# Hybrid decoder block on one core: the sixteen rows of modulation section 4 with four buffers, loaded ahead of their products

## The chip, the cores and the metric

The kernel runs on one core of one Trainium2 chip. The metric is the device time of one execution in microseconds, the median of several runs. The engines are named as the profile names them: PE is TensorE (its weight loads are PEld), DVE is VectorE, ACT is ScalarE, POOL is GpSimd, SP is SyncE, which here only issues transfers.

## The reference, cut to what matters

One layer of width 2048 over 512 positions, in f32. The vector `mod` has six sections of 2048; section 4 is the scale of the second norm.

```python
mod = jax.nn.silu(c) @ w_ada[l] + b_ada[l]
sh1, sc1, ga1, sh2, sc2, ga2 = jnp.split(mod, 6, axis=-1)
h = modulate(rmsnorm(x, g_mix_norm[l]), sh1, sc1)
proj = h @ w_in[l]
...
y = jnp.concatenate([rmsnorm(y_ssm, g_ssm_out[l]), rmsnorm(y_att, g_nsa_out[l])], axis=-1) @ w_out[l]
x = x + ga1[:, None, :] * y
h = modulate(rmsnorm(x, g_ffn_norm[l]), sh2, sc2)
x = x + ga2[:, None, :] * conv_ffn(h, w_up[l], conv_w[l], conv_b[l], w_down[l])
return rmsnorm(x, g_final)
```

`modulate(h, shift, scale)` is `h * (1 + scale) + shift`; `conv_ffn` is up projection, a causal convolution of width 3, gating, down projection.

## The kernel before

Activations lie transposed: 128 channels on the partitions, 512 positions along a row, so x is 16 tiles of 128 by 512. Every matrix product with exact weights is three matmuls (`mm3`, L100 to L102): a weight block is split by ACT into a rounded part `wh` (a cast) and by DVE into the rest `wl` (a subtraction), both L75, and the same is done to the activations (`yh`, `yl`).

The stages follow each other: `phase_a` and `phase_b1` (first modulation, input projection, state space part), `phase_b2` (attention, with the first half of the output projection as fill), `phase_c` (second half of the output projection, residual x, sums of squares), `up_first` and `up_rest` (up projection), `down`.

The change lies in `phase_c`. For its 16 output tiles it multiplies the attention half of the output projection's weights (`wout`) with `yh` and `yl`. The first two tiles (`first`) are made while DVE scales the last part of `yatt` by the norm's factor `rba` (L1055) and splits it. Two accumulators `mm` in PSUM are used in turn: the matmuls of tile n wait until `add` (L1043, on DVE) has read tile n-2 out of its accumulator into x, and for the `wl` and `wh` of their own tile, which have two places each as well. After `add`, ACT squares x (`cv`, L966), DVE adds the squares (L967), and a transfer on POOL's queue writes x to DRAM (`x2_d`, L1045).

In the same stage the 2048 numbers of section 4 are made: 16 rows of 128 numbers. For each row a block of w_ada (128 by 2048, f32, 1024 KB) is loaded into `adw`, DVE multiplies it with `silc` (silu of c, on every partition) and sums along the row (L124, result `adac`), and a one-column instruction (L333) writes `mod`. `adw` has two places. Rows 0 and 1 are loaded on SP's queue before the loop and multiplied there; the rest are loaded on POOL's queue, one behind each output tile, and the program text puts a row's product right behind its load.

All is written for one scheduler that orders each engine's instructions by the program's order and its own estimate of when inputs are there; each engine then works strictly in that order, and so does each queue of transfers. So an instruction that waits for its operand holds all that stands behind it on its engine. POOL's queue also holds the small power `rms_r` (L146) on which `rba` depends.

Of the kernel before, what the change touches and what calls it, by code (L numbers as in the profile page):

```python
# [10 lines left out]
F32 = mybir.dt.float32  # L11
# [3 lines left out]
ALU = mybir.AluOpType  # L15
# [3 lines left out]
P = 128  # L19
D = 2048  # L20
S = 512
KT = D // P
# [42 lines left out]
class Block:  # L65
# [262 lines left out]
    def ada_rest(self, sec, kt, pool=None, bufs=2, late=False):  # L328
        acc = self.cp.tile([P, 1], F32, name="adac", bufs=4)
        self.ada(sec, kt, acc, pool, bufs, late)  # L330
        o = self.mod[:, sec, kt:kt + 1]
        if sec == 4:
            self.V.scalar_tensor_tensor(o, acc, self.vec(V_GFFN + kt), self.mad[:, sec, kt:kt + 1],  # L333
                                        op0=ALU.mult, op1=ALU.add)
        else:
            self.V.tensor_add(o, acc, self.mad[:, sec, kt:kt + 1])
# [691 lines left out]
    def phase_c(self, x2, yatt, yh, yl, W, Wa, ps):  # L1028
        nc, tc, a, V, A, T = self.nc, self.tc, self.a, self.V, self.A, self.T

        Wa.tile([P, 2048], F32, name="adw", bufs=2)
        W.tile([P, S], F32, name="cv", bufs=CVB)
        W.tile([P, 8, P], F32R, name="rh", bufs=2)
        W.tile([P, 8, P], F32R, name="rl", bufs=2)
        na = sum(ADA) - 32
        for i in range(2):
            self.ada_rest(4, na, Wa, 2)
            na += 1
        for q in range(4):
            nc.sync.dma_start(x2[q], self.x_d[:, 4 * q:4 * q + 4])  # L1040
        def add(mt, p, sl):
            x = x2[mt // 4][:, mt % 4, sl]
            V.scalar_tensor_tensor(x, p, self.mod[:, 2, mt:mt + 1], x, op0=ALU.mult, op1=ALU.add)  # L1043
            self.add_square(self.acc2[:, sl], x, mt == 0, W)
            nc.gpsimd.dma_start(self.x2_d[:, mt, sl], x)  # L1045

        def first():

            w = self.weights(a["wout"][0, 1, 0])
            p = [ps.tile([P, S], F32, name="mm", bufs=2) for _ in range(2)]  # L1050
            for f in range(2):
                sl = slice(256 * f, 256 * f + 256)
                for k in range(8):
                    y = yatt[:, k, sl]
                    V.scalar_tensor_tensor(y, y, self.vec(V_GNSA + k), self.rba[f], op0=ALU.mult, op1=ALU.mult)  # L1055
                    self.split(y, yh[:, k, sl], yl[:, k, sl])
                    for e, (wh, wl) in enumerate(w):
                        self.mm3(p[e][:, sl], (wh[:, k], wl[:, k]), (yh[:, k, sl], yl[:, k, sl]), k == 0, k == 7)
            return p

        for u in range(7):
            for e, p in enumerate(self.wout_pair(u, 1, yh, yl, ps) if u else first()):
                add(2 * u + e, p, slice(0, S))
                if na < KT and 2 * u + e >= 0:
                    self.ada_rest(4, na, Wa, 2)
                    na += 1
        nc.sync.dma_start(self.taps, a["taps"])
        V.tensor_scalar(self.tapn, self.taps[:, NFF:, 0:3], -1.0, None, op0=ALU.mult)

        w = self.weights(a["wout"][3, 1, 1])  # L1070
        for f in range(2):
            sl = slice(256 * f, 256 * f + 256)
            for e, (wh, wl) in enumerate(w):
                p = ps.tile([P, 4, P], F32, name="tp", bufs=3).rearrange("p a b -> p (a b)")[:, sl]
                for k in range(8):
                    self.mm3(p, (wh[:, k], wl[:, k]), (yh[:, k, sl], yl[:, k, sl]), k == 0, k == 7)
                add(14 + e, p, sl)
                if f:
                    self.norm2(e, ps, W)
                    if e == 0:  # L1080
                        self.eps0 = self.rms_eps
# [457 lines left out]
```

## Time and profile before

| | |
|---|---|
| runs | 2338.4, 2343.06, 2365.14 us |
| median | 2343.06 us |
| profiled execution | 2354.09 us, its span 2352.3 us |
| busy in the span | PE 2195.6, PEld 1918.0, DVE 1854.9, ACT 1080.2, POOL 309.6 us |
| granted TensorE clock, mean | 0.967 of full speed |
| `phase_c`'s stretch, 846 to 947 us | PE 79.91, DVE 75.78, ACT 25.31 of 101 us |

The page of the profile gives busy time by engine and by group of instructions; the views used below are the waits (who waited for whom), the timeline of one engine, sums over given stretches, and the issues of transfers with the time until they landed. In a timeline a row is the start, the duration, the engine, the line, and in brackets the idle time ahead of it with what ended it; consecutive rows overlap in the pipeline, so the step from one start to the next is what an instruction costs.

### The profile page before, as it was taken

The page shows a single profiled execution, that of the slowest core. Times are in us where ns is not written, and L with a number is a line of the kernel's source. Part 1 is how long each engine was busy: PE and PEld are TensorE (multiplying, and loading weights), DVE is VectorE, ACT ScalarE, POOL GpSimd, SP SyncE. Part 2 cuts the span into 40 slices and gives each one's busy share as a digit, 9 for nine tenths or more (in the row PEclk, how much of TensorE's full clock was granted, in tenths as well). Part 3 has the DMA queues.
Part 4 walks back from the last instruction along what each step waited for, and adds up shares of the span by engine and source line. Part 5 has one row for each costly group of instructions (what it writes and reads, how often), then busy time and mean ns, then how long its engine had stood idle before and what let it go on. Part 6 is the DMA issues. An engine that isn't in the chain of part 4 may idle for free.

```text
span 2352.3 us, 34734 instructions
## 1 busy us (share of the span) xinstructions
PE 2195.6 (93%) x13694; PEld 1918.0 (82%) x13694; DVE 1854.9 (79%) x2776; ACT 1080.2 (46%) x1823; POOL 309.6 (13%) x376
## 2 busy tenths in 40 slices
PE   7997899878899878899999999999999999999997
PEld 5776778666677666899999999999999788888886
DVE  7896888658988877889999999999999773553436
ACT  3422444348867742744445444454444431221215
POOL 8999111100000011000000000000000000000000
PEclk9999999979999989999999999999999999999998
DMA  9784656576477467233333333333333783443223
GB/s 345 289 284 177 207 167 177 158 209 207 150 239 228 171 258 287 85 123 127 126 129 126 122 122 122 122 121 122 122 121 112 286 310 120 148 145 119 90 90 108
DMA packets 94003, 398.20 MB, mean 169 GB/s; under 512 B 19968, under 2 KB 28448, under 8 KB 58384
## 3 DMA queue, kind: packets, MB, share of 16 engines
q1 hardware_dynamic: 79440, 344.51, 42.0%
q0 software_dynamic: 14400, 51.49, 6.6%
q8 instruction: 107, 1.75, 0.3%
q14 instruction: 56, 0.46, 0.1%
HBM read 358.20 MB, written 37.69 MB: 168 GB/s over the span
## 4 chain that ended last, share of the span: by engine, by line
PE 54%; issue 4%; DVE 3%; ACT 1%; DMA 1%; POOL 1%; POOLq 0%; DVEq 0%; ACTq 0%
PE dn L102 7%; PE dn L100 7%; PE dn L101 6%; PE sa L101 6%; PE sa L100 6%; PE sa L102 6%; PE sb L100 5%; PE sb L102 5%; PE sb L101 5%; DMA adw<-in_wada_dram 0%; DVE wl L75 0%; DMA a_d<-cv 0%; POOL adw L119 0%; POOL x_d L1045 0%; DVE cv L1090 0%
## 5 line engine op out<-in xcount | busy, mean ns | idle before, releaser
L75 ACT CAST wh<-wr 128x1024 fp32r<-128x1024 f32 (+1 forms) x257 | 262.0, 1024 | 502.5 <-PE dn L101 320.5
L75 DVE TENSOR_TENSOR wl<-wr,wh 128x1024 fp32r<-128x1024 f32 (+1 forms) x255 | 307.6, 1210 | 50.1 <-ACT wh L75 38.8
L124 DVE SCALAR_TENSOR_TENSOR adw<-adw,silc 128x2048 f32<-128x2048 f32 x63 | 146.7, 2331 | 26.4 <-DMA adw<-in_wada_dram 25.3
L100 PE MATMUL mm<-yh,wh 128*128 128x512 f32 (+1 forms) x320 | 129.4, 409 | 26.7 <-DVE x L1043 7.8
L75 ACT CAST xh<-wq 128x1024 fp32r<-128x1024 f32 x84 | 88.3, 1052 | 139.2 <-DVE wq L1229 104.2
L75 ACT CAST wh<-wq 128x1024 fp32r<-128x1024 f32 x84 | 88.3, 1052 | 137.8 <-DVE wq L1229 104.5
L1099 POOL DMA_DIRECT2D a_d<-cv x44 | 23.8, 541 | 856.5 <-DVE cv L1098 856.5
L101 PE MATMUL mm<-yl,wh 128*128 128x512 f32 (+1 forms) x320 | 128.8, 403 | 7.4 <-DVE yl L75 7.4
L102 PE MATMUL mm<-yh,wl 128*128 128x512 f32 (+1 forms) x320 | 127.9, 401 | 1.9 <-DVE wl L75 1.9
L1293 DVE SCALAR_TENSOR_TENSOR x<-dn,mod,x 128x512 f32<-128x512 f32 (+1 forms) x56 | 37.6, 673 | 108.3 <-PE dn L102 107.8
L75 DVE TENSOR_TENSOR xl<-wq,xh 128x1024 fp32r<-128x1024 f32 x84 | 102.4, 1218 | 24.2 <-ACT xh L75 24.2
L75 DVE TENSOR_TENSOR wl<-wq,wh 128x1024 fp32r<-128x1024 f32 x84 | 102.2, 1218 | 22.7 <-ACT wh L75 22.7
L100 PE MATMUL dn<-b21h,wh 128*128 128x512 f32 x256 | 101.8, 398 | 3.1 <-ACT wh L75 3.1
L102 PE MATMUL dn<-b21h,wl 128*128 128x512 f32 x256 | 102.1, 399 | 0.5 <-DVE wl L75 0.5
L1229 DVE TENSOR_TENSOR wq<-wq,wr 128x1024 f32<-128x1024 f32 x84 | 102.0, 1215 | 0.1
L101 PE MATMUL dn<-b21l,wh 128*128 128x512 f32 x256 | 101.8, 398 | 0.0
L100 PE MATMUL dn<-t4h,wh 128*128 128x512 f32 (+1 forms) x256 | 97.8, 382 | 0.0
L102 PE MATMUL dn<-t4h,wl 128*128 128x512 f32 (+1 forms) x256 | 97.7, 382 | 0.0
L101 PE MATMUL dn<-t4l,wh 128*128 128x512 f32 (+1 forms) x256 | 97.6, 381 | 0.0
L100 PEld LDWEIGHTS mm<-yh,wh 128*128 128x128 f32 x320 | 62.7, 198 | 41.7 <-issue 16.9
L146 POOL TENSOR_TENSOR rms_r<-rms_v,mhalf 128x2 f32<-128x2 f32 (+1 forms) x8 | 10.8, 1346 | 637.5 <-DVE rms_v L144 637.4
L102 PE MATMUL mm<-hh,wl 128*128 128x512 f32 x192 | 79.5, 414 | 15.9 <-DVE wl L75 15.9
(535 smaller groups left out, 7852.8 us busy)
## 6 DMA issues: line engine op xcount, KB each, us to landing
adw<-in_wada_dram SPq DMA_DIRECT2D x49, 1024.0 KB, 6.7
wr<-in_wup_dram SPq DMA_DIRECT2D x46, 1024.0 KB, 4.9
wq<-in_wup_dram SPq DMA_DIRECT2D x42, 1024.0 KB, 6.8
wr<-in_wdn_dram SPq DMA_DIRECT2D x40, 1024.0 KB, 4.9
wr<-in_wada_dram SPq DMA_DIRECT2D x32, 1024.0 KB, 4.9
wr<-in_wout_dram SPq DMA_DIRECT2D x16, 1024.0 KB, 5.5
adw<-in_wada_dram POOLq DMA_DIRECT2D x14, 1024.0 KB, 7.7
wr<-in_wp_dram SPq DMA_DIRECT2D x12, 1024.0 KB, 5.2
```

The source lines that it names most:

```text
L75: return self.A.copy(hi, src), self.V.tensor_sub(lo, src, hi.bitcast(F32))
L100: self.T.matmul(ps, wh, xh, start=start, stop=False)
L101: self.T.matmul(ps, wh, xl, start=False, stop=False)
L102: self.T.matmul(ps, wl, xh, start=False, stop=stop)
L124: self.V.scalar_tensor_tensor(t, t, 1.0, self.silc, op0=ALU.mult, op1=ALU.mult, accum_out=out)
L146: self.rms_pow = self.nc.gpsimd.tensor_tensor(r[:, 0:n], v[:, 0:n], self.mhalf.to_broadcast([P, n]), op=ALU.pow)
L1099: self.nc.gpsimd.dma_start(self.a_d[:, m], val)
L1229: V.tensor_add(src, src, add)
L1293: V.scalar_tensor_tensor(x, p, gate, x, op0=ALU.mult, op1=ALU.add)
```

## The change

`adw` gets four places. Four rows are loaded before the loop, all on POOL's queue. Behind each output tile the oldest loaded row is multiplied and another is loaded; behind the last two tiles of the loop two rows are multiplied. The products and their number stay.

```diff
+    def ada_load(self, sec, kt, pool, bufs):
+        t = pool.tile([P, 2048], F32, name="adw", bufs=bufs)
+        self.nc.gpsimd.dma_start(t, self.a["wada"][sec, kt])
+        return sec, kt, t
+
+    def ada_row(self, sec, kt, t):
+        acc = self.cp.tile([P, 1], F32, name="adac", bufs=4)
+        self.V.scalar_tensor_tensor(t, t, 1.0, self.silc, op0=ALU.mult, op1=ALU.mult, accum_out=acc)
+        self.ada_out(sec, kt, acc)
...
-        Wa.tile([P, 2048], F32, name="adw", bufs=2)
+        Wa.tile([P, 2048], F32, name="adw", bufs=4)
...
-        for i in range(2):
-            self.ada_rest(4, na, Wa, 2)
-            na += 1
+        rows = []
+
+        def row():
+
+            nonlocal na
+            if na < KT:
+                rows.append(self.ada_load(4, na, Wa, 4))
+                na += 1
+
+        for i in range(4):
+            row()
...
                 add(2 * u + e, p, slice(0, S))
-                if na < KT and 2 * u + e >= 0:
-                    self.ada_rest(4, na, Wa, 2)
-                    na += 1
+                self.ada_row(*rows.pop(0))
+                if u == 6:
+                    self.ada_row(*rows.pop(0))
+                row()
```

`ada_out` holds the one-column instruction that stood in `ada_rest`. In the changed file L124 becomes L340 for these rows, L119 becomes L335, L333 becomes L346, L1043 becomes L1064, L1055 becomes L1076, L1045 becomes L1066.

On DVE, at the end of `first` and the first two tiles, the order before is this (`yatt` and `yl` are the last pieces of the scaled attention output, `adw,adac` is a row's product, `x_7650` the tiles of x):

```order
L75 TENSOR_TENSOR yl<-yatt,yh 128x256
L124 SCALAR_TENSOR_TENSOR adw,adac<-adw,silc 128x2048
L1055 SCALAR_TENSOR_TENSOR yatt<-yatt,vecs,rba_3953 128x256
L333 SCALAR_TENSOR_TENSOR mod<-adac,vecs,mad 128x1
L1055 SCALAR_TENSOR_TENSOR yatt<-yatt,vecs,rba_3953 128x256
L75 TENSOR_TENSOR yl<-yatt,yh 128x256 x2
L124 SCALAR_TENSOR_TENSOR adw,adac<-adw,silc 128x2048
L75 TENSOR_TENSOR wl<-wr,wh 128x1024 x2
L1043 SCALAR_TENSOR_TENSOR x_7650<-mm,mod,x_7650 128x512
```

Three products stand ahead of the first two `wl`; the third is that of row 2, whose load is issued behind the product of row 0. In the changed kernel the same place on DVE reads:

```order
L75 TENSOR_TENSOR yl<-yatt,yh 128x256 x3
L1076 SCALAR_TENSOR_TENSOR yatt<-yatt,vecs,rba_3953 128x256 x2
L340 SCALAR_TENSOR_TENSOR adw,adac<-adw,silc 128x2048
L75 TENSOR_TENSOR yl<-yatt,yh 128x256 x2
L346 SCALAR_TENSOR_TENSOR mod<-adac,vecs,mad 128x1
L340 SCALAR_TENSOR_TENSOR adw,adac<-adw,silc 128x2048
L75 TENSOR_TENSOR wl<-wr,wh 128x1024 x2
L1064 SCALAR_TENSOR_TENSOR x_7650<-mm,mod,x_7650 128x512 x2
L346 SCALAR_TENSOR_TENSOR mod<-adac,vecs,mad 128x1
L340 SCALAR_TENSOR_TENSOR adw,adac<-adw,silc 128x2048
L980 TENSOR_TENSOR acc_7654<-acc_7654,cv 128x512
```

Two products, of rows 0 and 1, stand ahead of the `wl`, and that of row 2 has moved behind the two `add`. Behind these rows the scheduler puts rows 3 and 4 ahead of the `add` of tile 2, so that by tile 11 all sixteen are done; the number of instructions on DVE is the same.

On POOL's queue the place around the last `rms_r` of the attention's norm reads before (`x_d<-z` and `x_d<-x_7650` are stores of x):

```order
L1009 DMA x_d<-z 128x512 x2
L146 TENSOR_TENSOR rms_r<-rms_v,mhalf 128x2
L119 DMA adw<-in_wada_dram 128x2048 x3
L1045 DMA x_d<-x_7650 128x512 x2
L119 DMA adw<-in_wada_dram 128x2048 x2
```

And in the changed kernel:

```order
L1022 DMA x_d<-z 128x512 x2
L335 DMA adw<-in_wada_dram 128x2048
L146 TENSOR_TENSOR rms_r<-rms_v,mhalf 128x2
L335 DMA adw<-in_wada_dram 128x2048 x5
L1066 DMA x_d<-x_7650 128x512 x2
```

The load of row 0 now stands on POOL ahead of `rms_r`, those of rows 1 to 5 behind it; on SP's queue the two loads that stood ahead of the four loads of x (L1040) are gone. PE's, ACT's and the rest of SP's order stay, but for one place: the two matmuls that spread `rms_r` stand eight small matmuls later on PE.

## Rows read from the trace of the kernel before

**Rows 1.** The page: busy time of PE over the span.

```profile
PE 2195.6 (93%) x13694; PEld 1918.0 (82%) x13694; DVE 1854.9 (79%) x2776; ACT 1080.2 (46%) x1823; POOL 309.6 (13%) x376
```

**Rows 2.** Stretches: us, busy of PE, PEld, DVE, ACT, POOL, PEclk, DMA share, GB/s.

```profile
846.00:947.00 101.00, 79.91 (x339) 63.65 (x340) 75.78 (x103) 25.31 (x36) 14.73 (x27) 0.90 0.74 274
...
1010.00:1780.00 770.00, 764.93 (x6620) 756.66 (x6619) 717.86 (x790) 382.14 (x438) 21.63 (x40) 1.00 0.34 124
...
866.00:947.00 81.00, 71.83 (x291) 56.66 (x292) 60.34 (x76) 20.22 (x26) 13.06 (x24) 0.94 0.73 271
```

**Rows 3.** Waits of PE, then of DVE, 846 to 950: total us, times, longest.

```profile
PE mm L100 <- DVE x L1043: 7.8, 1, 7.8
PE mm L100 <- DVE mod L333: 7.6, 2, 6.0
...
PE mm L102 <- DVE wl L75: 1.6, 1, 1.6
...
DVE adw L124 <- DMA adw<-in_wada_dram: 16.9, 7, 5.8
```

**Rows 4.** Timeline of DVE, 845 to 866.

```profile
845.29 1.28 DVE L1055 SCALAR_TENSOR_TENSOR yatt<-yatt,vecs,rba 128x256 f32<-128x256 f32 x3 [2.01 <-ACT rba L938]
846.48 1.09 DVE L75 TENSOR_TENSOR yl<-yatt,yh 128x256 fp32r<-128x256 f32 x3
847.49 1.27 DVE L1055 SCALAR_TENSOR_TENSOR yatt<-yatt,vecs,rba 128x256 f32<-128x256 f32 x3
...
860.60 2.29 DVE L124 SCALAR_TENSOR_TENSOR adw<-adw,silc 128x2048 f32<-128x2048 f32 x1 [4.46 <-DMA adw<-in_wada_dram]
...
862.82 2.35 DVE L75 TENSOR_TENSOR wl<-wr,wh 128x1024 fp32r<-128x1024 f32 x2
865.09 0.74 DVE L1043 SCALAR_TENSOR_TENSOR x<-mm,mod,x 128x512 f32<-128x512 f32 x1
```

**Rows 5.** Timeline of PE, 865 to 947.

```profile
865.98 0.77 PE L100 MATMUL mm<-yh,wh 128*128 128x512 f32 x1 [7.81 <-DVE x L1043]
...
869.67 0.39 PE L100 MATMUL mm<-yh,wh 128*128 128x512 f32 x1
...
933.62 0.77 PE L100 MATMUL mm<-yh,wh 128*128 128x512 f32 x1 [6.01 <-DVE mod L333]
...
937.60 0.39 PE L100 MATMUL mm<-yh,wh 128*128 128x512 f32 x1
...
946.70 0.28 PE L100 MATMUL tp<-yh,wh 128*128 128x256 f32 x1
```

**Rows 6.** Stretches of 2 us: PE busy, PEclk, DMA share, GB/s.

```profile
856.00:858.00 2.00, 2.00 (x10) 0.50 0.96 303
...
874.00:876.00 2.00, 2.00 (x11) 1.00 1.05 442
```

**Rows 7.** Timeline of POOL and of SP around the first loads.

```profile
843.36 0.72 POOL L146 TENSOR_TENSOR rms_r<-rms_v,mhalf 128x2 f32<-128x2 f32 x1 [8.72 <-DVE rms_v L144]
851.95 0.59 POOL L119 DMA_DIRECT2D adw<-in_wada_dram  x1 [7.88 <-issue]
...
836.83 0.91 SPq L119 DMA_DIRECT2D adw<-in_wada_dram  x2
```

**Rows 8.** Queues of transfers, 866 to 947: packets, MB, share of 16 engines' time.

```profile
q0 software_dynamic: 2722, 15.62, 51.2%
q1 hardware_dynamic: 864, 6.29, 21.4%
```

**Rows 9.** POOL's loads: landing of those at 851.95, 880.06, 919.59; time on POOL.

```profile
adw<-in_wada_dram POOLq DMA_DIRECT2D x1, 1024.0 KB, 8.6
...
adw<-in_wada_dram POOLq DMA_DIRECT2D x1, 1024.0 KB, 5.0
...
adw<-in_wada_dram POOLq DMA_DIRECT2D x1, 1024.0 KB, 9.8
...
L119 POOL DMA_DIRECT2D adw<-in_wada_dram x14: 537/539/587, 852.0 to 919.6; - x14
```

More of the change, by code (lines that the diff above doesn't have):

```diff
@@ L330, in ada_rest, with ada_out @@
         self.ada(sec, kt, acc, pool, bufs, late)
+        self.ada_out(sec, kt, acc)
[6 more added lines that the diff above has]
+        self.V.scalar_tensor_tensor(t, t, 1.0, self.silc, op0=ALU.mult, op1=ALU.mult, accum_out=acc)
+        self.ada_out(sec, kt, acc)
+    def ada_out(self, sec, kt, acc):
         o = self.mod[:, sec, kt:kt + 1]
```

## The prediction

> **What bounds the kernel now.** I read the page first: PE is busy for 93% of the span [rows 1], and in the long up projection for 764.93 of 770 us [rows 2]. So time is lost where PE stands, and `phase_c` is such a place: from 846 to 947 PE is busy for 79.91 of 101 us, at a mean clock of 0.90 [rows 2]. Work behind this stage follows PE and should move with it.
>
> Next the waits of PE in that stretch [rows 3]. The two long ones, 7.8 and 6.0 us, are both charged to DVE: in the first PE waits for the `add` of tile 0, which frees its accumulator, in the second for the `add` of tile 10. Two shorter ones of 1.6 us (the rest of the 7.6, and the wait for `wl`) are DVE's too. DVE itself waited 16.9 us for loads of `adw`, seven times, at most 5.8 us. The timeline of DVE shows how these hang together [rows 4]: the product of row 2 stands still for 4.46 us until 860.60, the two `wl` and the `add` of tile 0 (865.09) stand behind it, and PE starts at 865.98 [rows 5]. The load of that row was issued at 851.95 [rows 7], behind the product of row 0 whose place it takes, and took 8.6 us [rows 9]. The load at 919.59 took 9.8 us, and from that come the 5.8 us of DVE and the 6.0 us of PE.
>
> Each long wait costs twice: PE comes back at half its clock, which is 1.2 instead of 2.4 GHz (0.50 in 856 to 858 [rows 6]). At full clock a matmul of 512 columns costs 0.233 us (39 of them from 937.60 to 946.70). The nine from 865.98 to 869.67 took 3.69 us instead of 2.10, the nine from 933.62 to 937.60 took 3.98 [rows 5]: 1.6 and 1.9 us lost.
>
> **The start: tile 0 to the first matmul of tile 2.** Before, PE starts tile 2 at 865.98. In the changed order two products, not three, stand ahead of the `wl`, and neither waits if its row has landed. DVE then works without a stop from the arrival of `rba`, 845.29. From [rows 4]: three scalings of `yatt` in 1.19 us, so eight in 3.2; three `yl` in 1.01, so eight in 2.7; two products at 2.22 (860.60 to 862.82), 4.4; the two `wl` 2.27; a one-column step 0.1. That is 12.7 us, 858.0 for the start of the `add`. The spread of `rms_r` stands eight small matmuls later on PE; half of 0.233 each would be 0.9 us, but PE had been standing for `rms_r` there, so I take 0.3, with 0 and 0.9 as ends. The `add` begins at 858.3, and as PE followed it by 0.89 us before (865.09 to 865.98), tile 2 begins at 859.2. **Gain 6.8 us**; 6.2 to 7.1.
>
> Are the operands there? Row 0 stood on SP until 836.83 [rows 7], for transposes whose input lay in its place. On POOL its load waits for the same, and `rms_r`, now behind it, began at 843.36, so 6 us cover it. Row 0 is multiplied at about 850.8. Row 1 stands behind `rms_r`, is issued at 844.2, and must be there at 853.7: 9.5 us, where the loads shown took 5.0 to 9.8 [rows 9]. x is loaded on SP without the two rows ahead of it.
>
> **The loop: tiles 2 to 13.** Before, from 865.98 to 946.70 they take 80.7 us [rows 5]. 12 tiles of 24 matmuls at 0.233 are 67.2. The difference, 13.5, is 6.2 of gap ahead of 933.62, some 1.8 for each of the two short ones, 1.6 and 1.9 at half clock, and 0.2 left over. After, no gap should be left: rows are loaded four ahead, and DVE's work fits. In 866 to 947 DVE was busy for 60.34 us [rows 2] with 13 products; one more makes 62.6, less than 67.2. Going through the new order by these durations, the closest place is behind each pair of products (rows 6 and 7, rows 10 and 11), where `wl` and `add` still come about 2 us ahead of PE. PE still stands some 4.6 us ahead of tile 2, so I keep 1.7 us for a start at half clock: 68.9 us, end at 928.1. **Gain of the loop 11.8 us**, 18.6 with the start.
>
> **What the transfers allow.** The text says about three tiles from load to product; the scheduler pulls products forward, so row 4 is multiplied straight behind row 3, about 12 us behind its load (853.1 to 865.0). And the stage asks for the same bytes in less time. From [rows 8]: POOL's queue took 41.5 us (51.2% of 81) for 15.62 MB, 2.66 us each MB; SP's 17.3 us for 6.29 MB, 2.75 each. A row (1.05 MB) is 2.8 us, a weight block 2.9, a store of x 0.7. From 844, when row 1 is issued, to 914, when the product of row 15 would start, there are 15 rows (42 us), 5 weight blocks (14.5), 11 stores (7.7) and about 2 MB left of x (5.6): 69.8 us of work in 70. So the queues are as good as full. It may still fit, since row 15 can be 4 us late before PE notices, and since a share of 1.05 at 442 GB/s occurs [rows 6]. The cost of this lies between 0 and 4.5 us; I take 0.6, near the lower end, as PE has 2 to 4 us in hand at each place.
>
> Sum: 18.0 us. The profiled execution took 2354.09, 11 above the median; it would take 2336.1. From the median of 2343.06, **2325 us**. That is 0.8%; about 1%, 23.4 us, is what a measurement of this kernel can tell from no change, as its three runs spread over 27 us.
>
> **One rule against the change.** Two rows move from SP's queue to POOL's. The 14 loads on POOL took 537 to 587 ns each, beside an almost busy DVE [rows 9]. The Trainium skill, "SBUF — State Buffer", section "A bandwidth-pool intuition that's wrong (but worth ruling out)", says that a POOL-issued transfer of about 620 ns took about 3100 ns beside a DVE copy, since GpSimd can't write its descriptors until DVE releases the port that they share. By that row 1 would be issued and land about 2.6 us later, some of it behind DVE's demand, and the time would be up to 2327.6. The trace does not show it: the longest of the 14 is 587 ns.
>
> **Rivals.** *Rows late (0.22).* The full queues make DVE wait again, now for a backlog of three rows: row 4, then the second of each pair. For it: 69.8 in 70 us, and 303 GB/s at a share of 0.96 with two rows on POOL's queue [rows 6]. Against: each row is asked for only when an older product is done, so the backlog can't grow. Here too belongs row 1, if it lands at 844.2 + 14 instead of 9.5: 4.5 us at the start. Price 3 to 7 us: 2328 to 2332.
>
> *Slower: the transfers become the bound (0.04).* If a MB in this stretch costs not 2.7 but over 3.4 us (below about 295 GB/s), the 69.8 us become 88, the last product comes 18 us later, and all is given back; at 4 us, 103, it is 15 us slower: 2358. The 303 GB/s of one slice stand near that point, but 442 in another and 271 on average with idle time against it.
>
> *The change doesn't reach PE (0.06).* If the order of DVE leaves some other wait ahead of the `add` of tile 0 (x's own load, the `wout` block), the gaps move and stay: 2338 to 2345. Against it: before, 16.9 us of DVE's waits were for `adw` and none for these.
>
> *More than this (0.04).* If PE comes back at full clock and no load is late, 20.3 and a half more where the loads of the up projection come sooner: 2322.
>
> **How the numbers follow.** The forecast itself has 0.64, 2320 to 2330. Runs spread by some 6 us to each side of a median, so the range that holds 8 in 10 goes from 2314 to 2339: it takes in the rows that come late and leaves out the transfers as bound and half of the change that doesn't reach. Faster by over 1% (below 2319.6) needs a measurement 5 us below the forecast or the better case: 0.22. Slower by over 1%: 0.03. Within 1%: 0.75.
>
> **What would show it.** In the changed trace the `add` of tile 0 begins at about 858, PE starts tile 2 at about 859, no product of rows 0 to 2 waits for its load, and the small accumulators `tp` begin near 928 to 930. PE's waits on DVE in the loop (7.8, 6.0, 1.6, 1.6) shrink to one of some 4.6 ahead of tile 2; PE's clock is low once, not twice. The DMA share between 845 and 915 rises from 0.74 to over 0.9. Behind the stage every distance stays: the span behind the first `tp` was 2352.3 - 946.7 = 1405.6 us. I am wrong if the product of row 1 or row 4 stands for more than 3 us, if gaps of PE remain in the loop, or if a later stage takes back what this one gave.

## The result, and the profile after

The changed kernel takes 2334.43 us (median of 18 runs, 2326.87 to 2340.27), the kernel before, run beside it, 2349.7 us (18 runs, 2338.4 to 2365.14): a ratio of 0.9933, 95% interval 0.9918 to 0.9947, or 15.3 us less. The forecast was 2325 us (18.0 us less), the range 2314 to 2339. The profiled execution took 2332.81 us, its span is 2331.0 us.

Busy time of PE on the page, and then sums over stretches (columns as in [rows 2]); the stretch of `phase_c` first, then the time in which the rows are loaded:

```profile
PE 2186.7 (94%) x13694; PEld 1909.0 (82%) x13694; DVE 1855.1 (80%) x2776; ACT 1080.8 (46%) x1823; POOL 312.0 (13%) x378
```

```profile
846.00:947.00 101.00, 88.56 (x446) 73.92 (x446) 88.88 (x127) 34.40 (x51) 18.29 (x32) 0.95 0.78 303
...
845.00:915.00 70.00, 62.99 (x284) 51.15 (x285) 68.73 (x94) 21.46 (x30) 12.67 (x24) 0.95 0.94 369
```

In the kernel before, the second stretch reads:

```profile
845.00:915.00 70.00, 54.59 (x241) 43.52 (x240) 56.64 (x78) 17.46 (x26) 11.48 (x21) 0.90 0.83 312
```

In the same 101 us PE does 446 matmuls where it did 339 [rows 2], some of them the shorter ones of the work that follows. The waits of PE in this stretch show why (total us, times, longest; those of the norm behind the first `tp` are left out):

```profile
PE mm L100 <- DVE x L1064: 4.4, 1, 4.4
...
PE mm L101 <- DVE yl L75: 1.9, 2, 1.7
PE mm L100 <- ACT yh L75: 1.4, 1, 1.4
```

Of the four waits on DVE in [rows 3] one is left, 4.4 us ahead of tile 2; those for `yl` and `yh` belong to tiles 0 and 1 and stood before as well (1.8 and 2.7 us). And of DVE's own waits, 16.9 us for `adw` before, none is left at all: the view has no such line any more. The timeline of DVE shows the new start (compare [rows 4]):

```profile
844.77 1.28 DVE L1076 SCALAR_TENSOR_TENSOR yatt<-yatt,vecs,rba 128x256 f32<-128x256 f32 x3 [2.02 <-ACT rba L951]
...
849.96 2.29 DVE L340 SCALAR_TENSOR_TENSOR adw<-adw,silc 128x2048 f32<-128x2048 f32 x1
...
853.07 2.29 DVE L340 SCALAR_TENSOR_TENSOR adw<-adw,silc 128x2048 f32<-128x2048 f32 x1
...
855.29 2.36 DVE L75 TENSOR_TENSOR wl<-wr,wh 128x1024 fp32r<-128x1024 f32 x2
857.56 1.41 DVE L1064 SCALAR_TENSOR_TENSOR x<-mm,mod,x 128x512 f32<-128x512 f32 x2
...
859.01 2.29 DVE L340 SCALAR_TENSOR_TENSOR adw<-adw,silc 128x2048 f32<-128x2048 f32 x1
...
861.96 2.29 DVE L340 SCALAR_TENSOR_TENSOR adw<-adw,silc 128x2048 f32<-128x2048 f32 x1
...
864.16 2.29 DVE L340 SCALAR_TENSOR_TENSOR adw<-adw,silc 128x2048 f32<-128x2048 f32 x1
...
913.48 2.28 DVE L340 SCALAR_TENSOR_TENSOR adw<-adw,silc 128x2048 f32<-128x2048 f32 x1
```

Up to 866 no row has brackets behind it but the first: DVE never stands still here. The `add` of tile 0 comes 12.79 us behind the arrival of `rba` (857.56 - 844.77); before it was 19.80 (865.09 - 845.29). PE, from its timeline (compare [rows 5]), starts tile 2 at 858.45, is slow for nine matmuls (3.76 us until 862.21), and reaches the first `tp` at 927.31 without another gap:

```profile
858.45 0.77 PE L100 MATMUL mm<-yh,wh 128*128 128x512 f32 x1 [4.39 <-DVE x L1064]
...
862.21 0.39 PE L100 MATMUL mm<-yh,wh 128*128 128x512 f32 x1
...
927.31 0.28 PE L100 MATMUL tp<-yh,wh 128*128 128x256 f32 x1
```

The clock of these places, in stretches of 2 us (compare [rows 6]), is low once and not twice: it is back at full from 862 and stays there up to the first `tp`.

```profile
856.00:858.00 2.00, 0.00 (x0) 0.00 (x0) 2.00 (x3) 0.00 (x0) 0.21 (x1) 0.50 0.97 406
...
862.00:864.00 2.00, 2.00 (x10) 1.63 (x9) 2.00 (x2) 0.00 (x0) 0.15 (x1) 1.00 0.99 414
```

On POOL the load of row 0 is issued at 836.80, the rows 1 to 3 directly behind `rms_r`, and row 4 behind the product of row 0 (timeline of POOL, compare [rows 7]):

```profile
836.80 0.55 POOL L335 DMA_DIRECT2D adw<-in_wada_dram  x1 [2.67 <-PE pv L937]
842.84 0.72 POOL L146 TENSOR_TENSOR rms_r<-rms_v,mhalf 128x2 f32<-128x2 f32 x1 [5.49 <-DVE rms_v L144]
843.52 1.65 POOL L335 DMA_DIRECT2D adw<-in_wada_dram  x3
852.55 0.54 POOL L335 DMA_DIRECT2D adw<-in_wada_dram  x1 [7.38 <-DVE adw L340]
```

The load of row 1, issued at 843.52, with the time to its landing, and all sixteen loads with the time that their issue took on POOL:

```profile
adw<-in_wada_dram POOLq DMA_DIRECT2D x1, 1024.0 KB, 9.5
...
L335 POOL DMA_DIRECT2D adw<-in_wada_dram x16: 537/538/587, 836.8 to 896.9; - x16
```

Row 1 thus landed at about 853.05, and its product began at 853.07: no wait shows, but there was nothing to spare either. The rows 2 to 15 landed 2.4 us or more ahead of their products.

**Where the time came from.** The stage runs from the arrival of `rba` on DVE to the first `tp` on PE: 101.41 us before (845.29 to 946.70), 82.54 after (844.77 to 927.31), 18.87 less. Of these the start gave 7.01 (20.69 to 13.68 us from `rba` to tile 2) and the loop of twelve tiles 11.86 (80.72 to 68.86). The two profiled executions differ by 21.3 us in span, though: 0.5 was there when `rba` came, and behind the first `tp` the distance to the end is 1403.7 us for 1405.6. The experiments show that the other 2 us are no part of the change, and why the medians differ by 15 and not by 19.

### The profile page after: what moved, and what is told of

Its sections match the earlier page's. It is cut to its first block, busy times and chain, and to the rows that moved or that the text cites. A ratio compares the mean times of both kernels' runs of the same rounds, so it can differ in the third digit from the quotient of the medians.

```text
span 2331.0 us, 34737 instructions
## 1 busy us (share of the span) xinstructions
PE 2186.7 (94%) x13694; PEld 1909.0 (82%) x13694; DVE 1855.1 (80%) x2776; ACT 1080.8 (46%) x1823; POOL 312.0 (13%) x378
## 4 chain that ended last, share of the span: by engine, by line
PE 71%; DVE 11%; POOL 6%; ACT 4%; DMA 4%; issue 4%; SPq 0%; DVEq 0%; POOLq 0%; ACTq 0%
PE dn L102 6%; PE dn L100 6%; PE dn L101 6%; PE sa L100 6%; PE sa L101 6%; PE sa L102 6%; PE sb L100 5%; PE sb L102 5%; PE sb L101 5%; POOL sp L59 3%; PE mm L100 3%; PE mm L102 3%; PE mm L101 3%; DVE wl L75 2%; PE s L900 1%
## 5 line engine op out<-in xcount | busy, mean ns | idle before, releaser
L75 ACT CAST wh<-wr 128x1024 fp32r<-128x1024 f32 (+1 forms) x257 | 262.0, 1024 | 515.8 <-PE dn L101 320.7
L124 DVE SCALAR_TENSOR_TENSOR adw<-adw,silc 128x2048 f32<-128x2048 f32 x47 | 111.0, 2364 | 7.6 <-DMA adw<-in_wada_dram 6.4
L1309 DVE TENSOR_TENSOR x<-x,dn 128x512 f32<-128x512 f32 x32 | 22.0, 686 | 91.6 <-PE dn L102 91.6
```

Of the source, the lines that this page charges most:

```text
L75: return self.A.copy(hi, src), self.V.tensor_sub(lo, src, hi.bitcast(F32))
L124: self.V.scalar_tensor_tensor(t, t, 1.0, self.silc, op0=ALU.mult, op1=ALU.mult, accum_out=out)
L1309: V.tensor_add(x, x, p)
```

## The experiments

My theory: with two places a load is issued only behind the product of two rows before, so DVE waits for landings; in the start one product stood ahead of the `add` of tile 0 that had no need to. Rivals: only the order of the products counts, or only the number of places, or the queue that rows 0 and 1 are on; the transfers cost something that no wait shows, or set the end themselves.

All times of the stage are read as above, from the timelines of DVE and PE, in us behind the arrival of `rba`. The loop is the time from tile 2 to the first `tp`. Ratios are to the kernel before on the same chip.

| kernel | `add` 0 | tile 2 | first `tp` | loop | ratio, interval |
|---|---|---|---|---|---|
| before | 19.80 | 20.69 | 101.41 | 80.72 | |
| before_again | 17.52 | 18.41 | 97.57 | 79.16 | |
| before_third | 18.52 | 19.41 | 97.47 | 78.06 | |
| changed | 12.79 | 13.68 | 82.54 | 68.86 | 0.9933, 0.9918 to 0.9947 |
| changed_again | 12.68 | 13.57 | 82.76 | 69.19 | 0.9953, 0.9933 to 0.9973 |
| two_places | 12.68 | 13.57 | 91.25 | 77.69 | 0.9979, 0.9961 to 0.9997 |
| three_places | 12.69 | 13.58 | 82.64 | 69.06 | 0.9931, 0.9910 to 0.9952 |
| rows01_on_sp | 12.68 | 13.57 | 82.74 | 69.17 | 0.9930, 0.9910 to 0.9950 |
| four_places_old_text | 18.86 | 19.75 | 89.16 | 69.42 | 0.9981, 0.9962 to 0.9999 |
| four_places_old_text_again | 19.31 | 20.20 | 89.58 | 69.38 | |
| no_reload | 12.80 | 13.69 | 82.91 | 69.22 | 0.9934, 0.9901 to 0.9967 |
| rows_twice | 12.81 | 13.70 | 86.64 | 72.94 | 1.0026, 1.0005 to 1.0047 |
| adds_first | 7.05 | 8.03 | 76.01 | 67.98 | 0.9910, 0.9889 to 0.9932 |
| adds_first_again | 7.05 | 8.03 | 76.00 | 67.97 | 0.9912, 0.9894 to 0.9930 |

### Two places

```diff
-        Wa.tile([P, 2048], F32, name="adw", bufs=4)
+        Wa.tile([P, 2048], F32, name="adw", bufs=2)
...
-                rows.append(self.ada_load(4, na, Wa, 4))
+                rows.append(self.ada_load(4, na, Wa, 2))
...
-        for i in range(4):
+        for i in range(2):
             row()
...
                 if u == 6:
+                    row()
                     self.ada_row(*rows.pop(0))
```

> The changed kernel with two places of adw instead of four: two rows loaded ahead, each product two rows behind its load, so a load is again issued only behind the product of two rows before. DVE's order at the start is that of the changed kernel (the product of row 2 behind the add of tiles 0 and 1); in the loop products stand one tile later. My theory, that the lead of the loads makes the gain of the loop: the start keeps its 7 us (PE begins tile 2 at about 858.5), but pairs of rows follow each other at 10.1 us as before (860.60 to 921.31 for twelve rows), row 14 is multiplied at about 922 and the add of tile 10 behind it at about 925, so PE stands some 8 to 10 us in the loop and the first tp comes at 935 to 939; ratio to before 0.996 to 0.9975 (8 us slower than the changed kernel). Rival, that the order alone made the gain: no long wait, first tp within 2 us of 927.3, ratio 0.993 to 0.994. Rival, that only the number of places counts and the order nothing: PE begins tile 2 at 864 to 866 as before and the ratio is 1.000.

The start keeps all of its gain (13.57) and the loop almost none (77.69 for 78.06 to 80.72 before). DVE waits for rows again, as its timeline shows in two of five places:

```profile
871.71 2.29 DVE L340 SCALAR_TENSOR_TENSOR adw<-adw,silc 128x2048 f32<-128x2048 f32 x1 [1.92 <-DMA adw<-in_wada_dram]
...
921.77 2.29 DVE L340 SCALAR_TENSOR_TENSOR adw<-adw,silc 128x2048 f32<-128x2048 f32 x1 [3.26 <-DMA adw<-in_wada_dram]
```

So the start's gain comes from the order on DVE, which is the same here as in the changed kernel, and the loop's from the lead of the loads. The stage is 8.7 us longer than the changed kernel's, as the theory said; the ratio of 0.9979 lies a little above the 0.9975 that was named as its upper end. That the order alone makes the whole gain is excluded, and that the order does nothing as well.

### Three places

```diff
-        Wa.tile([P, 2048], F32, name="adw", bufs=4)
+        Wa.tile([P, 2048], F32, name="adw", bufs=3)
...
-                rows.append(self.ada_load(4, na, Wa, 4))
+                rows.append(self.ada_load(4, na, Wa, 3))
...
-        for i in range(4):
+        for i in range(3):
             row()
```

> The changed kernel with three places; DVE's order of instructions is the same as with four, only the loads from row 3 on are issued one product later. By the times of the changed kernel a load would then be issued 7.4 to 12 us ahead of its product, where loads took 6.8 to 14.5 (median 9.0). My theory (lead counts, and the queue of transfers shortens when fewer rows are asked for at once): DVE waits some 2 to 8 us for adw in all, PE loses 0 to 4 us, first tp at 927.5 to 931, ratio 0.993 to 0.995. If four places were needed for the whole gain (rows late whenever the lead falls under 9 us): first tp at 933 or later, ratio 0.996 or more.

The lower end of what was expected: 82.64 us and a ratio of 0.9931, no different from four places. Of the 2 to 8 us of waits for `adw` that were expected one is left, of 0.2 us:

```profile
DVE adw L340 <- DMA adw<-in_wada_dram: 0.2, 1, 0.2
```

The fourth place gives no time here, only slack: with three places the rows 5 and 7 land about 0.1 us or less ahead of their products. What it costs is space: 8 KB on every partition.

### Rows 0 and 1 on SP's queue

```diff
-        self.nc.gpsimd.dma_start(t, self.a["wada"][sec, kt])
+        q = self.nc.sync if kt < 2 else self.nc.gpsimd
+        q.dma_start(t, self.a["wada"][sec, kt])
```

> The changed kernel with the loads of rows 0 and 1 on SP's queue again, ahead of the loads of x; all else, DVE's order too, as changed. My theory: the queue counts for nothing here, first tp within 1 us of 927.3, ratio 0.9925 to 0.9945, the adds of tiles 0 and 1 don't wait for x. If moving the rows off SP's queue made part of the gain (x or the weight blocks earlier): PE's start of tile 2 1 us or more later and the ratio 0.995 or more. If POOL-issued loads beside DVE cost time, this is 1 to 3 us faster than the changed kernel, tile 2 at 858 or before.

82.74 us for 82.54 and 82.76, ratio 0.9930: the move of the two loads to POOL's queue is neither part of the gain nor a cost. It takes slack from row 1, though: on SP this load, issued at 848.54, took 6.8 us instead of 9.5, and its product began 7.3 us behind the landing:

```profile
adw<-in_wada_dram SPq DMA_DIRECT2D x1, 1024.0 KB, 6.8
```

### Four places and the old text

```diff
-        Wa.tile([P, 2048], F32, name="adw", bufs=2)
+        Wa.tile([P, 2048], F32, name="adw", bufs=4)
...
-            self.ada_rest(4, na, Wa, 2)
+            self.ada_rest(4, na, Wa, 4)
...
-                    self.ada_rest(4, na, Wa, 2)
+                    self.ada_rest(4, na, Wa, 4)
```

> The kernel before with one number changed: four places of adw instead of two; a row's product stays right behind its load in the text, rows 0 and 1 stay on SP. The scheduler then puts four products (rows 0 to 3) ahead of the first two wl and of the add of tile 0. My theory (the lead of the loads ends the waits of the loop; each product ahead of the add of tile 0 costs its 2.25 us): no wait for adw over 1 us, the add of tile 0 begins 12.8 + 2 x 2.25 = 17.3 us behind the arrival of rba (12.8 in the changed kernel, 19.8 before), and from rba to the first tp it is 87 us (82.5 in the changed kernel, 101.4 and 97.6 in the two traces of before); ratio 0.995. If the order of the text made the gain and not the places: 95 us or more, ratio 0.999 or more. If the two further products ahead of the add were free: 82.5 to 83.5 us, ratio 0.993.

This is the other half: the loop has all of its gain (69.42) and the start none (19.75). Four products now stand ahead of the `add` of tile 0, and the fourth waits for its row, which is issued only behind `rms_r`. So the start was 1.6 us longer than expected and the stage 89.2 us for 87. Since the ratio, 0.9981, tells less gain than the trace (89 for 97.5 to 101.4, some 0.4%), a second trace was taken:

> A second trace of the kernel with four places and the old text, whose ratio (0.998) was nearer to 1 than its first trace (89.2 us from rba to the first tp, some 10 under before) allows. If rows 2 and 3, which are issued only behind rms_r and multiplied ahead of the add of tile 0, wait for their landing by a varying time, this trace shows a wait of another length than 1.4 us at rows 2 or 3 and 88 to 95 us; if the trace is the same to 0.5 us, the ratio's interval is what is off.

The second trace gives 89.58. The timeline of DVE around the fourth product and the `add`:

```profile
864.79 2.29 DVE L124 SCALAR_TENSOR_TENSOR adw<-adw,silc 128x2048 f32<-128x2048 f32 x1 [1.82 <-DMA adw<-in_wada_dram]
...
867.01 2.35 DVE L75 TENSOR_TENSOR wl<-wr,wh 128x1024 fp32r<-128x1024 f32 x2
869.28 1.40 DVE L1043 SCALAR_TENSOR_TENSOR x<-mm,mod,x 128x512 f32<-128x512 f32 x2
```

The wait for row 3 is 1.8 us here and was 1.4 in the first trace, the rest is the same. By the traces (89.4 on average, 98.8 for the three of before) the ratio should be 0.996; the measured interval begins at 0.9962. What makes the small rest was not found and stays open; a varying landing of row 3 doesn't, as far as two traces tell.

### The transfers left out, and doubled

The first kernel leaves out the loads of rows 4 to 15; the second, which has three places, adds 13 loads that nobody needs:

```diff
+        tiles = []
...
-                rows.append(self.ada_load(4, na, Wa, 4))
+                rows.append(self.ada_load(4, na, Wa, 4) if na < 4 else (4, na, tiles[na % 4]))
+                if na < 4:
+                    tiles.append(rows[-1][2])
```

```diff
-        Wa.tile([P, 2048], F32, name="adw", bufs=4)
+        Wa.tile([P, 2048], F32, name="adw", bufs=3)
+        Wa.tile([P, 2048], F32, name="adx", bufs=2)
...
-                rows.append(self.ada_load(4, na, Wa, 4))
+                rows.append(self.ada_load(4, na, Wa, 3))
+                if na > 2:
+                    nc.gpsimd.dma_start(Wa.tile([P, 2048], F32, name="adx", bufs=2), a["wada"][3, na])
...
-        for i in range(4):
+        for i in range(3):
```

> The changed kernel without the loads of rows 4 to 15: the products stay and use the four loaded places over again (twelve of sixteen rows of section 4 are made from wrong numbers). DVE's order is the same. My theory (transfers are nearly full but nobody waits for them): from rba to the first tp 82.0 to 82.7 us against 82.5, ratio 0.992 to 0.994, DMA share of the stage down from 0.82 to about 0.4. If the transfers cost something that the waits don't show (slower DVE or PE beside them, weight blocks late): 80 us or less.

> Three places of adw, and behind each load of rows 3 to 15 a second load of 1024 KB on the same queue into another tile that nobody reads (13 more loads; the scheduler puts the late products further back on DVE). My theory: at 2.7 us each MB the stage then has 69.8 + 13 x 2.8 = 106 us of transfers from the issue of row 1 to the product of row 15, so this product starts some 105 us behind that issue (69 in the changed kernel), the scaling of x by section 4 waits for it, and the whole is 12 to 20 us slower than the changed kernel: ratio 0.998 to 1.002. If the queues had room that the shares don't show: row 15 within 80 us, ratio under 0.995. If the second loads also hold weight blocks and x: waits of PE in the loop and over 25 us lost.

Without twelve of the sixteen loads the stage takes 82.91 us, 0.2 above what was expected and as long as with them, and the ratio is the same 0.9934: the transfers cost nothing that the waits don't show. With 13 loads more the product of row 15 comes 107.4 us behind `rba` (68.7 in the changed kernel: 913.48 - 844.77), and the kernel is 22 us slower than the changed one (1.0026 for 0.9933), 2 more than the upper end named. Its trace, of the shortest of its ten runs, shows some 18 of them: 4.1 up to the first `tp` and 13.7 behind it. The sums over the stage, first without, then with the second loads (DMA share and GB/s are the last two numbers):

```profile
846.00:930.00 84.00, 76.71 (x346) 62.35 (x347) 77.06 (x104) 26.74 (x38) 7.47 (x14) 0.96 0.49 178
```

```profile
839.00:949.00 110.00, 92.94 (x441) 77.48 (x440) 83.88 (x113) 31.96 (x45) 24.26 (x45) 0.92 0.98 401
```

A share of 0.98 over 110 us, at 401 GB/s: this is what transfers as the bound look like. They take time mostly behind the loop (tile 2 to `tp` grows by 4 us only), where PE waits 9.9 us for a sum on DVE (2.7 in the changed kernel); that stands behind the scalings of x by section 4, and these behind the product of row 15 (946.88 to 949.16):

```profile
PE tp L142 <- DVE acc L980: 9.9, 1, 9.9
```

The changed kernel is near that point (0.94 from 845 to 915) and not past it. Row 15, issued at 925.68, landed 16.4 us later and so 4.8 us ahead of its product, which points to the order in which the scheduler then puts the last products as a part of the 9.9 us. How much is the order's and how much the transfers' was not separated by a run.

### The kernel before, again

Nothing is edited in these two.

> The kernel before once more, for a second trace of the same program. In the first trace the stage from the arrival of rba on DVE (845.29) to the first tp (946.70) took 101.4 us; in the changed kernel's trace 82.5. The medians differ by 15.3 us and not by 21. If the stage's waits for rows vary from run to run, this trace shows it in 95 to 101 us, with other lengths of the waits of DVE; if the stage is always 101 us, what is missing lies elsewhere, in stretches that the change doesn't touch.

> A third trace of the kernel before. From rba to the first tp 101.4 and 97.6 us so far. If landing times of loads make the length of the stage, this one lies between 93 and 102 us with other waits for adw than 16.9 and 12.3; mean gain of the change 14 to 17 us. If it is 101 again, the measured 15 us of the medians stay too small for the stage.

97.57 and 97.47 us from `rba` to the first `tp`, for 101.41 in the trace on which the prediction rests. The waits of before_again have this line for `adw`; for row 2, ahead of the `add` of tile 0, DVE stands by 2.18 us there and by 3.18 in the third trace, instead of 4.46:

```profile
DVE adw L124 <- DMA adw<-in_wada_dram: 12.3, 6, 4.0
```

```profile
866.38 2.29 DVE L124 SCALAR_TENSOR_TENSOR adw<-adw,silc 128x2048 f32<-128x2048 f32 x1 [2.18 <-DMA adw<-in_wada_dram]
...
857.77 2.29 DVE L124 SCALAR_TENSOR_TENSOR adw<-adw,silc 128x2048 f32<-128x2048 f32 x1 [3.18 <-DMA adw<-in_wada_dram]
```

The waits vary with the landing of loads, and the first trace had the longest ones. The mean of the three is 98.8 us, the mean of the changed kernel's two 82.65: 16.2 us, 0.7%, which is what the ratio 0.9933 says.

> The changed kernel again, beside adds_first on one chip. From rba to the first tp 82.5 to 83 us if the stage no longer depends on how fast loads land (three_places, rows01_on_sp and no_reload took 82.6, 82.7 and 82.9); ratio to before 0.9918 to 0.9947 as measured first.

The stage takes 82.76 us, within 0.4 us of all its relatives above. The ratio came out at 0.9953 on this chip (0.9933 to 0.9973), above what was expected; the intervals overlap, and by the two the gain is 11 to 16 us.

### The adds first

What is left in the start is one gap of 4.4 us and the half clock behind it. It stands behind two products and two `wl`, of which the `add` of tile 0 needs none.

```diff
-    def ada_row(self, sec, kt, t):
+    def ada_row(self, sec, kt, t, one=1.0):
         acc = self.cp.tile([P, 1], F32, name="adac", bufs=4)
-        self.V.scalar_tensor_tensor(t, t, 1.0, self.silc, op0=ALU.mult, op1=ALU.mult, accum_out=acc)
+        self.V.scalar_tensor_tensor(t, t, one, self.silc, op0=ALU.mult, op1=ALU.mult, accum_out=acc)
...
-                self.ada_row(*rows.pop(0))
+                if u == 0 and e == 0:
+                    continue
+                if u == 0:
+                    one = W.tile([P, 1], F32, name="one", bufs=1)
+                    V.tensor_scalar(one, x2[0][:, 1, 0:1], 0.0, 1.0, op0=ALU.mult, op1=ALU.add)
+                    self.ada_row(*rows.pop(0), one)
+                    row()
+                self.ada_row(*rows.pop(0), one if u == 0 else 1.0)
```

> The changed kernel with all products behind the adds of tiles 0 and 1: the products of rows 0 and 1 take their factor 1.0 from a column that is written out of tile 1 of x behind its add (one more small instruction on DVE), so they can't be put ahead of it. My theory (what is left of the start is DVE's: two products and two wl, 6.8 us, stand between the last yl and the add of tile 0, and PE waits 4.4 us there and comes back at half its clock for 1.7): the add of tile 0 begins 7 to 8 us behind rba instead of 12.8, PE has no gap over 2 us and stays at full clock; from rba to the first tp 76 to 79 us instead of 82.5; ratio 0.990 to 0.992. Rival (DVE's work in the loop is too much when two products more stand in it: 67 us of DVE in 67 us of PE): the gap comes back as waits of PE for wl or for adds later in the loop, 81 us or more, ratio 0.993.

> The kernel with the products behind the first two adds again. If its 6.5 us in the trace are real, its ratio is 0.0025 to 0.003 under that of the changed kernel beside it (0.990 to 0.9915), and from rba to the first tp it takes 75.5 to 77 us; if they are given back behind the stage, the two ratios are the same.

The timeline of DVE: the two `add` stand behind the last `yl`, then the two `wl`, then the new column, then the products.

```profile
858.26 1.41 DVE L1064 SCALAR_TENSOR_TENSOR x<-mm,mod,x 128x512 f32<-128x512 f32 x2 [0.89 <-PE mm L102]
859.58 2.35 DVE L75 TENSOR_TENSOR wl<-wr,wh 128x1024 fp32r<-128x1024 f32 x2
...
862.46 0.14 DVE L1089 TENSOR_SCALAR one<-x 128x1 f32<-128x1 f32 x1
862.63 2.35 DVE L340 SCALAR_TENSOR_TENSOR adw<-adw,one,silc 128x2048 f32<-128x2048 f32 x1
```

Now DVE waits for PE here (0.89 us) and not PE for DVE. The sums over the 84 us of the stage show PE busy for 82.73 of them at a clock of 1.00:

```profile
852.00:936.00 84.00, 82.73 (x412) 68.60 (x412) 79.70 (x111) 29.20 (x41) 15.24 (x28) 1.00 0.90 342
```

The stage takes 76.0 us in both traces, 6.7 less than the changed kernel, and the ratio is 0.9910 and 0.9912. Beside the changed kernel on one chip that is 0.9912 for 0.9953, 9.5 us between the medians, which is more than the trace shows; against the first ratio of the changed kernel, 0.9933, it would be some 5. The gap doesn't come back in the loop, though DVE has two more products in it. The median is 2326.94 and 2329.04 us, the shortest of all that ran.

## Why the prediction was right

**The start** was read rightly. Forecast were 13.0 us from `rba` to the `add` of tile 0 (858.3 - 845.29) and 0.9 more to tile 2; measured 12.79 and 0.89. The 0.3 us for the later spread of `rms_r` was not needed: `rba` reached DVE 1.93 us behind the start of `rms_r` before (843.36 to 845.29) and after (842.84 to 844.77). two_places shows that this gain is the order's alone. It has two parts. One is the wait for the row of the third product, 4.46, 2.18 and 3.18 us in the three traces of before. Without it each of the three takes 15.34 us from `rba` to the `add`, 2.6 more than the changed kernel's two, and of this the product itself is 2.22.

**The loop** came out at 68.86 us for a forecast of 68.9, with the half clock at 1.66 us (3.76 for 2.10) where 1.7 was put. The mechanism, that rows which are loaded ahead end DVE's waits, is shown by four_places_old_text, which has the lead without the order and the same loop (69.4), and by two_places, which has the order without the lead and a loop of 77.7. In the traces the two halves of the change add up: 5.9 us of start from the order, 8.7 to 9.9 of loop from the lead (two_places against the changed kernel, four_places_old_text against the mean of before, 79.3; the start's mean was 19.5). The 1.6 us by which two_places is under that mean are the order's too, or chance: the three loops of before differ by 2.7. The medians are too coarse to show the sum: by their ratios the halves give 4.9 and 4.5 us, 9.4 together, where the whole gives 11 to 16.

**The transfers** were put at 69.8 us of work in 70, with 0.6 us allowed for it. Row 1 was issued at 843.52 and row 15 multiplied at 913.48, 69.96 us, and no product waited: the 0.6 was not needed. The share of 845 to 915 is 0.94, as forecast (over 0.9); but it rises from 0.83 and not from 0.74, since the 0.74 that the text compared it with belonged to the longer stretch from 846 to 947. Of the rival that rows come late (0.22), the part on the backlog lost by a margin that three_places shows: even a place less gives only 0.2 us of waits. The part on row 1 lost by nothing: the text wanted this row within 9.5 us, near the end of the 5.0 to 9.8 that it had seen, and it took 9.53. It took 9.3 to 9.5 in every other trace that has the load on POOL and the product ahead of the `add`, so this repeats, but the text had no ground to expect it: that the start came out whole was close, and by the rows then known it was in part luck. The rival of the transfers as the bound is seen in rows_twice, with 13 loads more; at how many loads it begins was not run. Its price was set too high: there the last product came 38.7 us later than in the changed kernel and cost 22, where the text let each microsecond of delay cost one.

**The rule against the change**, of the Trainium skill, "SBUF — State Buffer", section "A bandwidth-pool intuition that's wrong (but worth ruling out)", on POOL-issued transfers that wait for their descriptors beside DVE, had no effect on the time: the 16 loads on POOL occupied it for 537 to 587 ns each in the changed kernel too, and with rows 0 and 1 on SP the stage was 82.74 us for 82.54. The Trainium skill tells it of a DVE copy; DVE here ran scalings, subtractions and products with two tensor operands. Row 1 did land later from POOL (9.5 us behind its issue, 6.8 from SP in rows01_on_sp), but whether that is the queue or the rows 2 and 3, which POOL issues directly behind it, no run separates; a load of 5.0 us that POOL issued beside a busy DVE [rows 9] speaks against a fixed delay.

**What was mis-sized** is the baseline, in two steps. The sum took each gap of before from one execution, in which the stage was the longest of three: 101.4 us where the mean is 98.8. This makes the gain of the stage 16.2 us where 18.6 was forecast ahead of the 0.6 for transfers, and the measured 15.3 fits that. The forecast time was then set against a median of three runs, 2343.06, where 18 runs give 2349.7; that is 6.6 of the 9.4 us between 2325 and 2334.4. From 2349.7 the same sum gives 2331.7. So the time lies outside the 2320 to 2330 to which the forecast itself gave 0.64, and above the 2328 to 2332 of the late rows, though no row was late; that it fell into the range is owed to the width that was put there for the spread of runs. The chance of 0.75 for a change within 1% fell on the right case.

"Behind the stage every distance stays" held for the work and not for the clock. The same instructions behind the first `tp` took 1403.7 us for 1405.6, but before_again took 1402.3 and before_third 1406.7, so this varies without the change (the last section shows where).

## What to carry to other kernels

Where a product waits for its own load, ask two things apart: how far the load runs ahead, and what stands behind the product on its engine. Here the lead was worth some 9 us and the order 6, each showed in its own stretch of the trace, and one place more than before gave the whole lead. Side work on an engine belongs behind whatever the bounding engine waits for, also when its operands are there long before; a scheduler that fills a gap with it may have to be kept from it by a dependence. And take the waits that a change is to remove from more than one trace: waits for transfers vary from run to run, while the two traces of the kernel without them agree to 0.2 us.

## What the runs showed of the hardware that was not expected

The core's 16 DMA engines moved 401 GB/s over 110 us at a share of 0.98 (rows_twice), while a row's load of 1024 KB took 9.0 us from issue to landing at the median in the changed kernel and 7.7 in the kernel before; in rows_twice it was 11.2. With more asked for at once each load took longer, and in the changed kernel nobody waited for it.

What a gap costs in clock is not settled by its length alone. Behind the stage, PE stands twice for a norm, by the same instructions in all kernels and with waits of the same length (6.1 to 6.2 us in all). In the first trace of the kernel before the clock fell in the first of these gaps already, in the changed kernel it stayed at full there; but it also stayed at full in before_again, which is the same program as before (sums over 5 us, the first trace of before, before_again, the changed kernel):

```profile
955.00:960.00 5.00, 2.93 (x19) 2.85 (x18) 4.63 (x9) 1.77 (x4) 1.52 (x2) 0.81 0.28 75
...
959.20:964.20 5.00, 2.93 (x27) 2.85 (x26) 4.60 (x9) 1.71 (x3) 1.52 (x2) 1.00 0.28 66
...
935.60:940.60 5.00, 2.85 (x26) 2.76 (x25) 4.57 (x9) 2.29 (x4) 1.60 (x2) 1.00 0.22 57
```

So this is no effect of the change. From the first `tp` to the up projection the stretch took 21.7, 19.3 and 21.8 us in the three traces of before, 20.2 and 20.5 in the two of the changed kernel. What decides whether the clock falls in such a gap these runs don't show.
